# Due times in estimated nanoseconds, not in instruction numbers, for the order of the engines around TensorE

## Chip, core and metric

The kernel runs on one core of a Trainium2 chip. The metric is the device time of one execution in microseconds (us); lower is better. TensorE (PE in the profile; PEld is its weight load) has its instructions in the order of the program; VectorE is DVE, ScalarE is ACT, GpSimd is POOL, and SyncE (SP) issues all DMAs.

## What is computed

One step of a two-layer streaming encoder for 2048 new frames (the prompt) and 8 running streams of 16 frames. Layer A is a gated DeltaNet with 8 heads, layer B is RWKV-7 with 16 heads of 64. Both have a large input projection, a recurrence over time that is evaluated in blocks, and an output projection:

```python
h = rms_norm(x, norm_w[i])
# layer A
proj = h @ w_in                                   # 1024 -> 6160
qkv = silu(causal_conv(proj[..., :CONV_CH]))
o, s = gated_delta_rule(q, k, v, beta, g, s0)     # S_t = a_t S + k_t u_t^T
y = (rms_norm(o) * silu(z)) @ w_out               # 2048 -> 1024
# layer B
xs = h + (h_shifted - h) * mu                     # six mixes
r, k, v, z = xs[:4] @ w_in                        # 4 x (1024 -> 1024)
S = S * w_t + sa * b_t + v_t * k_t                # per head, per frame
y = ((group_norm(o) + bonus) * silu(z)) @ w_out
x = x + y
```

## The kernel before

**Tiling.** Tokens lie along the free dimension, channels along the 128 partitions. Layer A goes through five blocks of tokens (384 or 512 columns; the first holds the 8 running streams too), layer B through six (384 columns, the first 256). Each large product is made in 32-bit through splits: a weight pair `whl` and an activation pair hold a rounded part and the rest, and three matmuls replace one (L451 to L453 in layer A's input projection, L1059 to L1061 in layer B's, L168 to L170 in both output projections). ACT rounds (`L124` for weights, `L162` for activations), and DVE or POOL subtracts (`L125`, `L163`). A weight pair that is made once is stored to DRAM (`wd`, L128) and loaded from there for later blocks (`load_w`, L133); there are six slots for pairs of the input projections, two for those of the output projections.

**The order of TensorE** is written out by hand. Generators for the projection (the stream), the recurrences and the output projection are interleaved by `weave` and `rounds`, step by step: while TensorE goes through the projection of a later block, the small matmuls of the recurrences stand between. In layer B a step handles one pair of heads in 12 rounds: `b_prep`, `b_subst` (a 16x16 triangular inverse on DVE, 30 dependent operations at L842 and L844, then two hops through DRAM, `sc2b<-TB` and `cm<-sc2b`), `b_inverse` (POOL spreads the hopped blocks into `T`, L1265; matmuls at L1281 and on), `b_scan` (the recurrence: matmul L1390, DVE `XV` at L1392, matmul L1379 of the next chunk), `b_gate`, `b_out`. Layer A has the same parts (`T` at L655, first used at L705; the triangular merges down to L744). The transition, in which layer A's last heads run beside layer B's first projections, lies between.

**The order of the other engines** is left to a planner. `MANUAL` (L33) keeps TensorE in program order. For DVE, ACT, POOL and SP the planner runs through the program on a clock of its own, and each time an engine is free it takes, of the instructions that are ready then, the one with the lowest priority number; the lists that come out are then executed in order on the chip. The priority numbers come from `_due` (L1580). The program is built twice: the first time `note` (L1627) writes a log of all instructions, `_due` goes through the log from its end, and in the second build L1631 sets `tc.cur_priority` to each instruction's due.

In `_due`, a matmul that stands as number j in the log has due j. Any other instruction is due at the smallest of: its own number plus `SLACK` (300); the `need` of what it writes; the `free` of the buffers that it holds up (the due of the instruction that writes the next tile of the ring). Whoever feeds an instruction must be `LEAD` (6) numbers earlier, or `LEAD_DMA` (40) where the instruction is a DMA. So time is counted in instructions of all engines, whatever each takes.

Of the kernel before, what the change touches and what calls it, by code (L numbers as in the profile page):

```python
# [10 lines left out]
F32R = mybir.dt.float32r  # L11
AF = mybir.ActivationFunctionType
ALU = mybir.AluOpType
# [3 lines left out]
P = 128  # L17
# [13 lines left out]
WRAW, WHL = {"w": 3, "o": 2}, {"w": 6, "o": 2}  # L31
PSUM = {"mm": 2, "g": 3, "o": 1, "r": 2}
MANUAL = {mybir.EngineType.PE}  # L33
LEAD, LEAD_DMA, SLACK = 6, 40, 300
AHEAD, PACE, LAST_PACE, ROUNDS = 101, 17, 8, 12
EXPC = 0.5 * math.exp(-0.5)
B_BO, B_MK, B_MS, B_M16, B_B4, CB_W = 0, 128, 384, 448, 512, 516
# [1535 lines left out]
@with_exitstack  # L1573
def tile_hybrid_gdn_rwkv7_stream_step(ctx: ExitStack, tc: tile.TileContext, io: dict):
    k = _K(ctx, tc, io)
    k.setup()
    k.layers()


def _due(log):  # L1580


    ring, before, first = {}, {}, {}
    for j, (_, _, outs, _) in enumerate(log):
        for name, tag, bufs in outs:
            if tag is not None and name not in first:
                first[name] = j
                r = ring.setdefault(tag, [])
                r.append(name)
                if bufs and len(r) > bufs:  # L1590
                    before[name] = r[-1 - bufs]
    need, free, due = {}, {}, [0] * len(log)
    for j in range(len(log) - 1, -1, -1):
        engine, dma, outs, ins = log[j]
        wrote = [o[0] for o in outs]
        if engine == mybir.EngineType.PE:
            d = j
        else:
            d = min([j + SLACK] + [need[t] for t in wrote if t in need] + [free[t] for t in ins + wrote if t in free])
        due[j] = max(0, d + LEAD_DMA)  # L1600
        d -= LEAD_DMA if dma else LEAD
        for t in ins + [t for t in wrote if first.get(t) != j]:
            need[t] = min(need.get(t, d), d)
        for t in wrote:
            if first.get(t) == j and t in before:
                free[before[t]] = min(free.get(before[t], d), d)
    return due


def _build(arrays, due=None):  # L1610

    import concourse.bacc as _bacc

    nc = _bacc.Bacc("TRN2", target_bir_lowering=False, num_devices=1)
    io = {}
    for name, a in arrays.items():
        io[name] = nc.dram_tensor(f"in_{name}", a.shape, mybir.dt.from_np(a.dtype), kind="ExternalInput").ap()
    for name, shape in _OUTS.items():
        io[name] = nc.dram_tensor(f"out_{name}", shape, F32, kind="ExternalOutput").ap()
    log = []  # L1620

    def tiles(aps):
        ts = [getattr(getattr(a, "bass_ap", None), "tensor", None) for a in aps]
        return [(t.name, getattr(t, "tag", None), getattr(getattr(t, "tag_meta", None), "bufs", None)) for t in ts if t is not None]

    with tile.TileContext(nc) as tc:
        def note(inst, *_):  # L1627
            if due is None:
                log.append((inst.engine, "DMA" in type(inst).__name__, tiles(inst.outs), [t[0] for t in tiles(inst.ins)]))
            else:  # L1630
                tc.cur_priority = due[len(log)]  # L1631
                log.append(None)

        nc.push_inst_callback(note)
        tile_hybrid_gdn_rwkv7_stream_step(tc, io)
        nc.pop_inst_callback()
    return nc, log
# [31 lines left out]
```

## Time and profile before

| what | value |
|---|---|
| time, median of 3 runs | 4665.8 us (4654.6 to 4667.97) |
| the profiled execution, its own time | 4661.34 us |
| its span, first to last instruction | 4659.5 us |
| mean granted TensorE clock, share of full speed | 0.955 |
| PE busy | 4343.3 us, 93% |
| DVE busy | 3470.7 us, 74% |
| ACT busy | 2290.0 us, 49% |
| POOL busy | 1735.8 us, 37% |

A busy share is a mean over the whole span. TensorE's order is fixed, so its time is its matmuls, at the clock that is granted, and its waits.

### The profile page before, as it was taken

The numbers are of one execution on the slowest core, as the hardware profiler recorded it, in microseconds if no ns is written. First come the engines' busy times: TensorE is split into PE (matmuls) and PEld (weight loads), VectorE is DVE, ScalarE is ACT, GpSimd is POOL, SyncE is SP. The second block draws the span as 40 slices with busy tenths as digits, with TensorE's granted clock in tenths as the row PEclk, the third lists the DMA queues.
The fourth block names the chain that finished last, engine by engine and source line by source line (L and its number), as shares of the span: only waits on it lengthen the run. The fifth ranks groups of instructions, "written<-read, shape, count | busy, mean of one in ns | idle before, by whom it ended". The sixth has DMA issues, their size and how long they took to land. (4 is left out here: it accounts for less than half of the span.)

```text
span 4659.5 us, 104081 instructions
## 1 busy us (share of the span) xinstructions
PE 4343.3 (93%) x37093; PEld 3733.9 (80%) x37093; DVE 3470.7 (74%) x9203; ACT 2290.0 (49%) x6132; POOL 1735.8 (37%) x2507
## 2 busy tenths in 40 slices
PE   7999999999999999999987889999999999999996
PEld 6788788888888899999986767778787887887775
DVE  6778766686666766767678888877778778777784
ACT  5444544554434444444456655555545446445542
POOL 6555443332111211211103455444434434344441
PEclk8888999999999999999998989999999999999997
DMA  5555665555555666666655666766665665665442
GB/s 189 183 179 177 221 211 177 180 188 157 174 145 146 182 206 185 191 209 185 188 153 173 202 204 215 225 189 188 193 199 162 203 203 165 202 194 148 139 131 70
DMA packets 765670, 842.18 MB, mean 181 GB/s; under 512 B 263480, under 2 KB 497360, under 8 KB 765152
## 3 DMA queue, kind: packets, MB, share of 16 engines
q1 hardware_dynamic: 765152, 835.53, 59.5%
q8 instruction: 294, 4.82, 0.4%
q14 instruction: 224, 1.84, 0.1%
HBM read 632.73 MB, written 202.53 MB: 179 GB/s over the span
## 5 line engine op out<-in xcount | busy, mean ns | idle before, releaser
L451 PE MATMUL ps<-hh,whl 128*128 128x384 f32 (+1 forms) x1960 | 804.7, 411 | 12.4 <-ACT hh L162 10.3
L452 PE MATMUL ps<-hl,whl 128*128 128x384 f32 (+1 forms) x1960 | 718.2, 366 | 2.5 <-DVE hl L163 2.0
L453 PE MATMUL ps<-hh,whl 128*128 128x384 f32 (+1 forms) x1960 | 717.3, 366 | 2.7 <-POOL whl L125 2.7
L1059 PE MATMUL ps<-xh,whl 128*128 128x384 f32 (+1 forms) x1632 | 608.4, 373 | 32.8 <-ACT xh L162 19.0
L1060 PE MATMUL ps<-xl,whl 128*128 128x384 f32 (+1 forms) x1632 | 561.1, 344 | 21.3 <-POOL xl L163 12.4
L1061 PE MATMUL ps<-xh,whl 128*128 128x384 f32 (+1 forms) x1632 | 559.3, 343 | 9.9 <-DVE whl L125 9.6
L125 POOL TENSOR_TENSOR whl<-wraw,whl 128x256 fp32r<-128x256 f32 x454 | 365.9, 811 | 414.4 <-ACT whl L124 389.8
L571 DVE SCALAR_TENSOR_TENSOR cv<-pre,cw,cv 128x512 f32<-128x512 f32 (+3 forms) x576 | 375.3, 659 | 124.8 <-ACT cv L569 117.8
L124 ACT CAST whl<-wraw 128x256 fp32r<-128x256 f32 x726 | 287.8, 402 | 313.2 <-PE ps L453 94.4
L451 PEld LDWEIGHTS ps<-hh,whl 128*128 128x128 f32 x1960 | 377.4, 193 | 69.3 <-issue 18.5
L168 PE MATMUL ps<-oh,whl 128*128 128x384 f32 (+2 forms) x1024 | 392.1, 383 | 27.7 <-DMA whl<-wd 14.9
L453 PEld LDWEIGHTS ps<-hh,whl 128*128 128x128 f32 x1960 | 376.5, 192 | 39.6 <-POOL whl L125 4.2
L452 PEld LDWEIGHTS ps<-hl,whl 128*128 128x128 f32 x1960 | 378.2, 193 | 35.4 <-DVE hl L163 5.8
L1059 PEld LDWEIGHTS ps<-xh,whl 128*128 128x128 f32 x1632 | 322.1, 197 | 76.4 <-ACT xh L162 25.3
L169 PE MATMUL ps<-ol,whl 128*128 128x384 f32 (+2 forms) x1024 | 368.5, 360 | 6.9 <-DVE ol L163 6.7
L170 PE MATMUL ps<-oh,whl 128*128 128x384 f32 (+2 forms) x1024 | 365.3, 357 | 0.7 <-POOL whl L125 0.7
L842 DVE TENSOR_TENSOR sbt<-B,TB 48x15 f32<-48x15 f32 (+14 forms) x1320 | 346.5, 262 | 23.6 <-DMA B<-scr 2.8
L844 DVE TENSOR_TENSOR TB<-TB,sbt 48x15 f32<-48x15 f32 (+14 forms) x1320 | 347.6, 263 | 19.6
L1060 PEld LDWEIGHTS ps<-xl,whl 128*128 128x128 f32 x1632 | 325.1, 199 | 33.1 <-POOL xl L163 16.8
L1061 PEld LDWEIGHTS ps<-xh,whl 128*128 128x128 f32 x1632 | 323.6, 198 | 18.4 <-DVE whl L125 17.8
L820 DVE TENSOR_TENSOR x<-x,ps 128x384 f32<-128x384 f32 (+1 forms) x320 | 191.3, 598 | 91.1 <-PE ps L170 90.7
L168 PEld LDWEIGHTS ps<-oh,whl 128*128 128x128 f32 x1024 | 198.7, 194 | 66.6 <-ACT oh L162 9.6
(349 smaller groups left out, 10268.4 us busy)
## 6 DMA issues: line engine op xcount, KB each, us to landing
whl<-wd SPq DMA_DIRECT2D x1582, 256.0 KB
wd<-whl SPq DMA_DIRECT2D x428, 256.0 KB
wraw<-in_w_a SPq DMA_DIRECT2D x288, 128.0 KB
wraw<-in_w_b SPq DMA_DIRECT2D x256, 128.0 KB
kvd<-kvo SPq DMA_DIRECT2D x160, 192.0 KB
xn<-x1d SPq DMA_DIRECT2D x80, 192.0 KB
wraw<-in_w_ao SPq DMA_DIRECT2D x96, 128.0 KB
xn<-in_x SPq DMA_DIRECT2D x32, 256.0 KB
```

The source lines that it names most:

```text
L125: (self.nc.gpsimd if tag == "o" else self.weng).tensor_tensor(w[:, 1], raw, w[:, 0].bitcast(F32), op=SUB)
L168: self.nc.tensor.matmul(out, lhsT=wh, rhs=hh, start=first and i == 0, stop=False)
L169: self.nc.tensor.matmul(out, lhsT=wh, rhs=hl, start=False, stop=False)
L170: self.nc.tensor.matmul(out, lhsT=wl, rhs=hh, start=False, stop=i == n - 1)
L451: nc.tensor.matmul(p, lhsT=wh[:, k % 2], rhs=hh, start=k == 0, stop=False)
L452: nc.tensor.matmul(p, lhsT=wh[:, k % 2], rhs=hl, start=False, stop=False)
L453: nc.tensor.matmul(p, lhsT=wl[:, k % 2], rhs=hh, start=False, stop=k == KT - 1)
L571: nc.vector.scalar_tensor_tensor(o, f(j), self.cw[:, ct, j:j + 1], o, op0=MUL, op1=ADD)
L844: nc.vector.tensor_tensor(T[:, j + 1:16, 0:j + 1], T[:, j + 1:16, 0:j + 1], o, op=SUB)
L1059: nc.tensor.matmul(o, lhsT=wh[:, i], rhs=xh, start=k == 0, stop=False)
L1060: nc.tensor.matmul(o, lhsT=wh[:, i], rhs=xl, start=False, stop=False)
L1061: nc.tensor.matmul(o, lhsT=wl[:, i], rhs=xh, start=False, stop=k == KT - 1)
```

## The change

`LEAD_DMA` goes. Each log entry now carries an estimated duration in nanoseconds (`_cost`): for DVE, ACT and POOL a constant and a rate per element of a partition, with 1200 more for a power; for a DMA 4000 and 0.04 per element; for a matmul 0.46 per column in the split products, else by its size. The matmuls' estimated durations added up give a clock (`at`); a matmul's due is its place on that clock. Any other instruction's due is the smallest of its place plus 40,000 ns, the needs and the frees, less its own duration, so it is a latest start. What feeds a matmul must be 1000 ns ahead of it; what feeds another instruction must be done at that one's latest start. Where dues below zero were cut off at zero, all dues are now shifted so that the smallest is zero. Nothing else differs: the same instructions, tiles, buffers and TensorE order.

```diff
-LEAD, LEAD_DMA, SLACK = 6, 40, 300
+LEAD, SLACK = 1000, 40000
+DMA_COST, POW_COST = (4000, 0.04), 1200
+COST = {mybir.EngineType.DVE: (280, 0.95), mybir.EngineType.Activation: (250, 1.0), mybir.EngineType.Pool: (300, 2.2)}
...
+def _cost(inst):
+
+    outs, ins = [[tuple(p.shape) for p in (getattr(a, "bass_ap", None) for a in aps) if p is not None] for aps in (inst.outs, inst.ins)]
+    if "DMA" in type(inst).__name__:
+        return DMA_COST[0] + DMA_COST[1] * max([math.prod(s) for s in outs + ins] + [0])
+    n = max([math.prod(s[1:]) for s in outs + ins] + [1])
+    if inst.engine != mybir.EngineType.PE:
+        a, b = COST.get(inst.engine, (100, 0))
+        return a + b * n + (POW_COST if getattr(inst, "op", None) == ALU.pow else 0)
+    k, m = ins[1][0], math.prod(ins[1][1:])
+    n = math.prod(ins[0][1:])
+    if ins[0] and inst.ins[0].bass_ap.dtype == F32R:
+        return 0.46 * n
+    return max(30 + 1.5 * n * k * m / (P * P), 200 if k * m == P * P else 0)
...
+    at, now = [], 0.0
+    for engine, cost, _, _ in log:
+        at.append(now)
+        now += cost if engine == mybir.EngineType.PE else 0
...
-        engine, dma, outs, ins = log[j]
+        engine, cost, outs, ins = log[j]
...
         if engine == mybir.EngineType.PE:
-            d = j
+            d = at[j]
         else:
-            d = min([j + SLACK] + [need[t] for t in wrote if t in need] + [free[t] for t in ins + wrote if t in free])
-        due[j] = max(0, d + LEAD_DMA)
-        d -= LEAD_DMA if dma else LEAD
+            d = min([at[j] + SLACK] + [need[t] for t in wrote if t in need] + [free[t] for t in ins + wrote if t in free]) - cost
+        due[j] = d
+        if engine == mybir.EngineType.PE:
+            d -= LEAD
...
-    return due
+    low = min(due)
+    return [int(d - low) for d in due]
...
-                log.append((inst.engine, "DMA" in type(inst).__name__, tiles(inst.outs), [t[0] for t in tiles(inst.ins)]))
+                log.append((inst.engine, _cost(inst), tiles(inst.outs), [t[0] for t in tiles(inst.ins)]))
```

## Rows read from the trace of the kernel before

**Rows 1.** The page's head: span, and busy time of each engine.

```profile
span 4659.5 us, 104081 instructions
...
PE 4343.3 (93%) x37093; PEld 3733.9 (80%) x37093; DVE 3470.7 (74%) x9203; ACT 2290.0 (49%) x6132; POOL 1735.8 (37%) x2507
```

**Rows 2.** Busy time and granted clock in five stretches of the span.

```profile
core 0: us, PE busy (x) PEld busy (x) DVE busy (x) ACT busy (x) POOL busy (x), PEclk, DMA share, GB/s
0.00:500.00 500.00, 448.12 (x2470) 388.12 (x2471) 379.46 (x982) 239.59 (x654) 289.60 (x488) 0.89 0.58 185
500.00:2330.00 1830.00, 1798.15 (x11049) 1572.61 (x11048) 1267.99 (x3238) 815.54 (x2047) 456.96 (x741) 1.00 0.61 183
2330.00:2800.00 470.00, 396.81 (x3168) 335.46 (x3166) 380.31 (x1168) 285.93 (x824) 178.32 (x285) 0.90 0.59 183
2800.00:4543.00 1743.00, 1620.81 (x19433) 1373.56 (x19433) 1384.85 (x3663) 914.26 (x2496) 789.32 (x965) 0.95 0.63 184
4543.00:4660.00 117.00, 79.43 (x986) 64.14 (x982) 58.09 (x157) 34.69 (x112) 21.62 (x28) 0.78 0.24 70
```

**Rows 3.** Waits of PE: whom for, us in total, times, longest.

```profile
PE ps L1379 <- DVE XV L1392: 43.7, 38, 2.6
PE ps L744 <- DVE T L739: 22.3, 18, 1.4
...
PE ps L1281 <- POOL T L1265: 17.5, 5, 7.3
...
PE ps L1060 <- POOL xl L163: 12.4, 12, 4.1
...
PE ps L705 <- POOL T L655: 7.9, 2, 6.5
...
PE ps L106 <- POOL OC L1473: 5.2, 1, 5.2
PE ps L1185 <- POOL ch L1158: 4.2, 2, 3.6
```

**Rows 4.** Timeline of one wait in layer B, in order of start.

```profile
4276.05 3.48 POOL L1178 TENSOR_TENSOR BK<-ch,ch 64x384 f32<-64x384 f32 x3
...
4278.58 1.24 DVE L1099 TENSOR_TENSOR w<-w2r,w 64x256 fp32r<-64x256 f32 x1
...
4279.85 0.60 DVE L1392 SCALAR_TENSOR_TENSOR XV<-ps,wc,Sw 64x64 f32<-64x64 f32 x2
...
4280.18 0.59 PE L1379 MATMUL ps<-XV,GM 128*64 128x64 f32 x3 [2.27 <-DVE XV L1392]
```

**Rows 5.** Busy times and granted clock just after that wait.

```profile
4281.80:4288.60 6.80, 6.80 (x70) 5.22 (x68) 4.55 (x19) 1.47 (x5) 0.83 (x1) 0.50 0.23 62
```

**Rows 6.** The chain of waits in layer B: start, us, what.

```profile
3588.38 0.17 PE ps L1059
...
3588.90 1.54 PE ps L1281 x48
```

**Rows 7.** Instruction groups by shape: busy us, mean ns, idle before.

```profile
L842 DVE TENSOR_TENSOR sbt<-B,TB 48x15 f32<-48x15 f32 x80 | 23.5, 294 | 2.4 <-DMA B<-scrb 1.3
...
L1392 DVE SCALAR_TENSOR_TENSOR XV<-ps,wc,Sw 64x64 f32<-64x64 f32 x416 | 116.6, 280 | 82.2 <-PE ps L1390 70.8 <-PE ps L1395 3.3
...
L1265 POOL TENSOR_TENSOR T<-cm,cb 128x384 f32<-128x384 f32 x80 | 67.8, 855 | 125.3 <-DMA cm<-sc2b 76.8 <-PE ps L1345 35.8 <-DVE GM L1213 4.1
```

**Rows 8.** DMAs on the chain of waits in layer B: start, us from issue to landing.

```profile
3441.53 4.54 DMA whl<-wd
...
3622.53 3.60 DMA cm<-sc2b
...
4323.90 4.13 DMA sc2b<-TB
```

**Rows 9.** Waits of SP's DMA queue, the longest in total.

```profile
SPq L133 <- PE ps L453: 528.6, 453, 3.2
```

**Rows 10.** One DVE line: duration ns min/median/max, first and last start.

```profile
L1099 DVE TENSOR_TENSOR w<-w2r,w x48: 421/976/1416, 2491.2 to 4463.3; 64x256 fp32r<-64x256 f32 x48
```

## Prediction

> **What bounds the kernel now.** I read the page's head first. TensorE is busy for 4343.3 of 4659.5 us and DVE, the next, for 3470.7 [rows 1]. So no other engine sets the time by its sum; the time is TensorE's fixed list, plus its waits of 4659.5 - 4343.3 = 316 us, plus what a lowered clock costs. The table by stretches says where these lie [rows 2]. Span less PE busy gives 52 us of idle time up to 500 us (layer A's first block), 32 in the long rest of layer A, 73 in the transition, 122 in layer B, 38 at the end. Its PEclk column, one minus it times the length, gives 55, 0, 47, 87 and 26 us of clock lost, 215 in all. Layer A after 500 us is therefore full: 1798 of 1830 us at full clock. All that another order can gain lies in the other four stretches.
>
> The two losses go together. Before the matmul at 4280.18 us TensorE waited 2.27 us [rows 4], and in the stretch from 4281.8 to 4288.6 us, in which it was busy throughout, the granted clock was 0.50 of full speed, 1.2 GHz in place of 2.4 [rows 5]. Over the span 215 us of clock go with 316 us of waits, so I count 0.68 us of clock for each us of wait that is saved or added, which is an estimate from these two sums.
>
> Then whom TensorE waits for [rows 3]. The costliest single wait is on `XV` (43.7 us in 38 times), the step of layer B's recurrence. POOL is waited for in five rows: `T` 17.5 and 7.9, `xl` 12.4, `OC` 5.2, `ch` 4.2, 47.2 us together, which is much for an engine that is busy 37% of the span [rows 1]. An engine that is free so often and is yet waited for has done its work in the wrong order, or got its input late. The wait on L739 (22.3 us in 18 times, never over 1.4) is of another kind: a matmul, a copy and the next matmul, with too little between; an order can't shorten that.
>
> **The change part by part.** It adds and removes no instruction, so busy sums stay, and TensorE's list stays. What moves is the order on DVE, ACT, POOL and SP, and only where the planner has more than one instruction ready.
>
> *The unit.* Without DMAs there are 26,557 instructions in layer B's 1743 us, 15.2 per us, and 17,075 in the 1830 us of full layer A, 9.3 per us [rows 2]. The old lead of 6 numbers is thus 0.39 us in layer B and 0.64 us in layer A on average, and it stretches and shrinks: split matmuls start each 0.17 us, so 6 of them take 1.0 us, while 48 small matmuls take 1.54 us, so 6 of those take 0.19 us [rows 6]. Behind such a burst the old rule gives nearly no lead, and layer B's recurrence and inverse are made of bursts.
>
> *DVE and ACT.* The new price of `XV` is 280 + 0.95 x 64 = 341 ns (it took 280), that of a 48x15 step of the inverse 294 ns (it took 294) [rows 7]. With the 1000 ns before the matmul, `XV` must start 1.34 us ahead of its matmul where it was due 0.39 us ahead. But in the wait that I looked at, DVE ran `w` (1.24 us) for a matmul of the next step when `XV` became ready [rows 4]; no due helps if `XV` was not ready when `w` was picked. Bounds: nothing, and half of the 43.7 us. I take a quarter, 10.9 us, since most of its waits are a single operation long (43.7 / 38 = 1.15 us).
>
> *POOL.* 384 elements now cost 300 + 2.2 x 384 = 1145 ns (`T` took 855 [rows 7]) against 0.39 us: here the old price was furthest off, two to three times too low. Work that feeds TensorE through POOL gets its place earlier by about 0.75 us for each POOL step. Bounds: nothing, and all of the 47.2 us. Some of it is a late DMA before the POOL operation, since `T` sat idle 76.8 us for `cm` [rows 7]. I take half, 23.6 us.
>
> *SP and the hops.* A hop of `cm` is priced at 4000 + 0.04 x 12,288 = 4.5 us (it took 3.60), the one of `sc2b` at 5.0 (4.13), a load of a weight pair at 4000 + 0.04 x 65,536 = 6.6 us (4.54) [rows 8]; each was 40 numbers, 2.6 us in layer B. The chain of `subst` (30 steps, a copy, two hops, `T`) was due to start some 272 numbers, 18 us, ahead of its matmul; now it is 9.7 + 0.5 + 9.5 + 1.1 + 1.0 = 22 us. That helps the waits on `T` and stands in the POOL term. Against it, a load is now ordered by its latest start, 7.6 us before its matmul, and a `cm` hop 6.6 us before that of `T`; before, the hop was 6 numbers (0.4 us) ahead of the load. Loads overtake hops. SP stands at L133 1.17 us at a time until TensorE frees a slot (528.6 / 453 [rows 9]), and all that is behind it stands too. Bounds: nothing, and two such waits (`sc2b`, `cm`) in each of layer B's 48 pairs of heads, 2 x 1.17 x 48 = 112 us. I take nothing, because the waits of `T` on TensorE's side are 5 in number [rows 3] and the hops start 4 us earlier; the upper end is a rival below.
>
> *At no cost.* The shift to a smallest due of zero changes no order but at the start, where 52 us of idle time are all there is. The slack goes from 300 numbers, 25 us at 54,935 instructions in 4659.5 us [rows 1], to 40 us: it postpones stores that nobody needs, and a store that holds a buffer is still bound by its `free`. If that cover went, it would show as SP's waits.
>
> *The sum.* 10.9 + 23.6 = 34.5 us of waits, with clock 34.5 x 1.68 = 58 us: 4661.3 - 58 = 4603 us on the profiled run's clock. That run lies 4.5 us under the median of the runs, so I say 4605 us, 1.3% faster.
>
> **A rule against it.** DVE's `w` has two inputs in SBUF, and one shape took 421, 976 and 1416 ns (least, median, most) [rows 10]; in the wait above it took 1.24 us beside a POOL operation that ran from 4276.05 to 4279.53 [rows 4]. The Trainium skill (SBUF — State Buffer, Who interferes with whom) says that a DVE instruction with two SBUF inputs contends with a GpSimd instruction that reads SBUF, and that the second one is blocked for the whole instruction. By that rule no fixed price per element fits DVE; the trace agrees, as the price for 256 elements is 523 ns. What it would make of the time is the third rival.
>
> **The rivals.**
> 1. *Nothing to pick.* With one instruction ready at a time the due doesn't matter; the wait at 4280 is of that kind, and DVE's 74% leave room. Against it: POOL's 47 us. The order still shifts a little and the time ends within 14 us of before: 4666.
> 2. *Loads ahead of hops.* A third of the 112 us reaches TensorE, since `T` is now the longest chain into it: 37 x 1.68 = 63 us, 4661 + 63 = 4724, and with the 4.5 us 4728, slower. It decides from 34.5 us on, where it eats the gains. For it: 76.8 us that POOL already sits for `cm`; against it: only 17.5 of them get to TensorE.
> 3. *DVE prices too low where POOL runs.* POOL's work moves earlier, into stretches where DVE is due; operations take 1.24 us that are priced 0.52, and `XV` stands behind them. If its waits double (43.7 us) and POOL's half is gained, 20.1 us are added, x 1.68 = 34: 4700, slower. It decides from 23.6 us of added DVE waits on.
>
> **How the numbers follow.** My forecast has 0.50, its own range 4545 (all of POOL's waits and half of `XV`'s: 69 x 1.68 = 116 us) to 4651. Rival 1 has 0.21, rival 2 0.17, rival 3 0.12. A measurement of this kernel can't tell less than about 0.3%, 14 us, from no change. Faster by more than that has 0.51 (a little of rival 1's edge), within it 0.20, slower 0.29. The range for 8 in 10 is 4530 to 4725: a little under the forecast's best case, up to most of rival 2.
>
> **What would show it.** Right: POOL's five rows of waits fall from 47 to about 24 us, `XV` to some 33, PE idle to about 280 us, mean clock above 0.955 with the gain in the transition and layer B, and the stretch from 500 to 2330 us of the same length within 10 us. Wrong: `T` <- `cm` waits rise on POOL and on TensorE (rival 2); mean durations of DVE's two-input operations rise with waits on `XV` (rival 3); the same rows with the same counts (rival 1). Wrong altogether if the long layer A stretch opens up, where TensorE waits little now and so has 32 us to win and much to lose.

## The result, and the profile after

The changed kernel took 4682.4 us (median of 6 runs, 4675.2 to 4690.7), the kernel before beside it 4662.5 us (6 runs, 4648.4 to 4668.0). The ratio is 1.0051, with a 95% interval of 1.0032 to 1.0071: half a per cent slower, where 1.3% faster was predicted. Run once more beside other kernels (e8) it gave 1.0050 (1.0033 to 1.0066). The profiled execution took 4690.7 us.

The head of its page, to set beside [rows 1]:

```profile
span 4688.9 us, 104185 instructions
...
PE 4335.9 (92%) x37093; PEld 3739.2 (80%) x37093; DVE 3481.4 (74%) x9203; ACT 2290.3 (49%) x6132; POOL 1719.0 (37%) x2507
```

The list of work is the same. Span less PE busy was 316 us and is now 353. Two of the five stretches of [rows 2]:

```profile
core 0: us, PE busy (x) PEld busy (x) DVE busy (x) ACT busy (x) POOL busy (x), PEclk, DMA share, GB/s
...
500.00:2330.00 1830.00, 1811.08 (x11073) 1583.57 (x11072) 1258.78 (x3241) 812.81 (x2047) 448.49 (x740) 0.99 0.61 183
2330.00:2800.00 470.00, 372.86 (x3044) 322.85 (x3042) 367.97 (x1119) 274.60 (x795) 160.39 (x266) 0.88 0.57 178
...
```

In the transition PE is busy for 24 us less than before in the same 470 us and gets through 3044 matmul records where it got through 3168. The waits of PE over the whole span, whose names answer to those of [rows 3] (every line number is two higher):

```profile
PE ps L1381 <- DVE XV L1394: 47.5, 44, 2.6
PE ps L1283 <- POOL T L1267: 31.3, 7, 7.8
PE ps L1436 <- DVE VS L1407: 18.5, 10, 2.8
PE ps L1062 <- POOL xl L165: 16.4, 9, 4.2
PE ps L889 <- DVE TB L846: 15.9, 5, 4.1
...
PE ps L1187 <- POOL ch L1160: 14.2, 4, 6.5
PE ps L170 <- ACT oh L164: 12.6, 11, 1.4
PE ps L746 <- DVE T L741: 11.0, 17, 4.1
PE ps L707 <- POOL T L657: 10.7, 2, 9.6
...
PE ps L1061 <- ACT xh L164: 6.8, 6, 2.2
```

and before, the rows that [rows 3] leaves out:

```profile
PE ps L1059 <- ACT xh L162: 19.0, 16, 2.4
...
PE ps L1061 <- DVE whl L125: 9.6, 20, 1.2
...
PE ps L1434 <- DVE VS L1405: 7.8, 4, 2.5
...
PE ps L887 <- DVE TB L844: 3.6, 1, 3.6
...
PE ps L168 <- ACT oh L162: 3.5, 6, 1.2
```

Four rows on POOL rose (`T` 17.5 to 31.3 and 7.9 to 10.7, `xl` 12.4 to 16.4, `ch` 4.2 to 14.2), and `XV` rose by 3.8. Three rows on other engines rose by as much together: `TB` by 12.3, `VS` by 10.7, `oh` by 9.1. Of the rows above 9 us three fell to less than half: `xh` (19.0 to 6.8) and `whl` (9.6 to 0.2), the inputs and the weights of layer B's projection, and the one on L741, of which the prediction said that no order could shorten it. In a second execution of the changed kernel (e8) each of the rows shown lies within 3 us of these.

TensorE's list of work being the same, the two traces can be laid on each other: for each matmul, when it started less when the same matmul started before. The growth of that difference in seven stages (bounds in time of the kernel before), for all kernels of this study, from one profiled execution each:

```
us won (-) or lost (+)  6-683 683-2327 2327-2453 2453-2683 2683-2963 2963-3547 3547-4651
changed kernel          +10.5    -17.4      -1.9     +31.3      +0.4     -10.3     +16.5
the same, again (e8)     -2.9    -17.5      +2.1     +28.1      -1.7      -9.5     +12.3
e1 ring out              +6.7    -18.0      +3.9     +10.4     +10.0      -7.2     +12.6
e2 before, long lead     -2.9     +5.4      +4.6     +20.6      -2.8      -3.6      +4.7
e3 load 10 us           +10.3    -15.2      +1.2     +26.1      +1.7     -10.0     +15.9
e4 equal prices          -1.7     -6.4      +2.0      +9.1     +10.1     -12.8     +10.3
e5 loads early          +10.3    -16.9      +1.8     +21.1     +20.7      -8.8     +13.1
e6 casts early           +9.1    -15.5      +2.8     +21.7      -1.2      -9.4     +15.9
e7 two orders            +7.1    -15.0      +3.4      +1.7      +7.4     -10.1     +10.0
e9 late reductions       +4.0    -16.4      -0.6      -0.1      -0.7      -2.4      +6.8
e10 prices on numbers    +6.2    -18.3      +3.7      +7.5      -5.0     -15.6      -4.0
e11 window               -4.2    -16.6      -0.3      +1.9      -3.0      -9.7      +5.0
e12 measured axis, out   -0.1    -17.6      -0.6      +3.3      -0.1     -10.1     +22.3
e13 measured axis        -8.3    -13.6      +1.1     +11.8      -2.5      -8.5     +11.7
```

The two rows of the same kernel show how far one execution can be read: 1 to 4 us in most stages, 13 in the first. Three more runs test this: behind 2453 us, e9 and e11 have the order of before on every engine, and so has e2 from 3547 us on. What their rows show there, -9.7 to +6.8 us, isn't order. All three show a loss in the last stage (+4.7 to +6.8), so the profiled execution of before was itself some 5 us short there. The profiled executions of e4, e8 and e13 were the shortest of their 12, that of e5 the longest of 6, so the sum of a row isn't the ratio. The stages before 683 and after 2963 say little alone. Two stages are clear: **the steady part of layer A wins 17 us, and 2453 to 2683 us, layer B's first chunks, loses 28 to 31.**

**The gain.** DVE's timeline around the copies of one step of the inverse, before (start, duration, line, operation):

```profile
1646.15 0.54 DVE L621 TENSOR_REDUCE sm<-QT 128x3 f32<-128x384 f32 x1
1646.73 0.25 DVE L738 TENSOR_SCALAR T<-ps 32x96 f32<-32x96 f32 x1
1647.01 0.27 DVE L622 TENSOR_SCALAR sm<-sm 128x3 f32<-128x3 f32 x1
1647.31 0.25 DVE L739 TENSOR_SCALAR T<-ps 32x96 f32<-32x96 f32 x1
...
1648.16 0.26 DVE L739 TENSOR_SCALAR T<-ps 32x96 f32<-32x96 f32 x1
```

and after:

```profile
1650.72 0.25 DVE L740 TENSOR_SCALAR T<-ps 32x96 f32<-32x96 f32 x1
1650.98 0.24 DVE L741 TENSOR_SCALAR T<-ps 32x96 f32<-32x96 f32 x1
1651.24 0.26 DVE L740 TENSOR_SCALAR T<-ps 32x96 f32<-32x96 f32 x1
1651.52 0.26 DVE L741 TENSOR_SCALAR T<-ps 32x96 f32<-32x96 f32 x1
...
1652.93 0.55 DVE L623 TENSOR_REDUCE sm<-QT 128x3 f32<-128x384 f32 x1
```

Four copies that TensorE waits for had the small operations of another chain laid between them, from 1646.73 to 1648.42; now they run through in 1.06 us.

**The loss.** PE's waits in 2453 to 2640 us after:

```profile
PE ps L1187 <- POOL ch L1160: 12.8, 2, 6.5
PE ps L1122 <- DVE w L1101: 8.2, 1, 8.2
PE ps L1283 <- POOL T L1267: 7.8, 1, 7.8
PE ps L1061 <- ACT xh L164: 6.8, 6, 2.2
```

Before, the wait on `w` was there too (8.7), `T` had 4.9 and `ch` nothing. One of the two waits on `ch` on ACT's timeline after, up to the operation that POOL's `ch` needs:

```profile
2521.38 0.39 ACT L126 CAST whl<-wraw 128x256 fp32r<-128x256 f32 x1
2521.67 0.69 ACT L1010 ACTIVATE xt<-H,mu 128x128 f32<-128x128 f32 x2
2522.27 0.40 ACT L126 CAST whl<-wraw 128x256 fp32r<-128x256 f32 x1
2522.56 0.41 ACT L164 CAST xh<-xt 128x256 fp32r<-128x256 f32 x1
2522.87 0.51 ACT L1153 ACTIVATE ch<-K,prm 128x256 f32<-128x256 f32 x1
```

The same `ch<-K` ran at 2514.07 before. What stands ahead of it now are casts of weights and of the inputs of coming matmuls. TensorE isn't ready for many of these weights: ACT's waits in 2440 to 2650 us after begin with

```profile
ACT whl L126 <- PE ps L1063: 26.7, 25, 4.5
ACT whl L126 <- DMA wraw<-in_w_b: 20.4, 20, 3.2
```

where ACT's casts before waited 1.7 us for TensorE, and for their loads

```profile
ACT whl L124 <- DMA wraw<-in_w_b: 33.6, 35, 2.0
```

A cast that waits for TensorE has its data and wants a buffer that TensorE still reads: it came too early, and ACT stood with all that was behind it.

**A first theory.** `_due` passes a due time back through a ring of buffers as well (`free`). A raw weight load is now priced at 4000 + 0.04 x 32,768 = 5.3 us, its cast and subtraction at half a us each: 6.3 us for one trip round three buffers. TensorE uses three pairs there in some 2 us of the planner's axis, so each trip puts loads and casts 4 us further ahead of need. Worked out with the kernel's own planner, the due of a cast lies 56 us (median), at most 112, ahead of its place in layer B's first block, and was behind it before. The rival theories: other prices put layer B's chains late, or the early loads themselves stand in SP's queue (the prediction's second rival).

### The profile page after: what moved, and what is told of

It is laid out like the page before. It is cut to its first block, busy times and chain, and to the rows that moved or that the text cites. A ratio compares the mean times of both kernels' runs of the same rounds, so it can differ in the third digit from the quotient of the medians.

```text
span 4688.9 us, 104185 instructions
## 1 busy us (share of the span) xinstructions
PE 4335.9 (92%) x37093; PEld 3739.2 (80%) x37093; DVE 3481.4 (74%) x9203; ACT 2290.3 (49%) x6132; POOL 1719.0 (37%) x2507
## 5 line engine op out<-in xcount | busy, mean ns | idle before, releaser
L1062 PE MATMUL ps<-xl,whl 128*128 128x384 f32 (+1 forms) x1632 | 558.0, 342 | 23.0 <-POOL xl L165 16.4
L844 DVE TENSOR_TENSOR sbt<-B,TB 48x15 f32<-48x15 f32 (+14 forms) x1320 | 356.6, 270 | 37.2 <-DMA B<-scr 12.4
L846 DVE TENSOR_TENSOR TB<-TB,sbt 48x15 f32<-48x15 f32 (+14 forms) x1320 | 346.8, 263 | 22.3
L1062 PEld LDWEIGHTS ps<-xl,whl 128*128 128x128 f32 x1632 | 323.4, 198 | 31.0 <-POOL xl L165 19.2
```

The costliest lines, as they stand in the source:

```text
L844: nc.vector.tensor_tensor(o, B[:, j + 1:16, j:j + 1].to_broadcast([rows, m, j + 1]), T[:, j:j + 1, 0:j + 1].to_broadcast([rows, m, j + 1]) ...
L846: nc.vector.tensor_tensor(T[:, j + 1:16, 0:j + 1], T[:, j + 1:16, 0:j + 1], o, op=SUB)
L1062: nc.tensor.matmul(o, lhsT=wh[:, i], rhs=xl, start=False, stop=False)
```

## The experiments

**e1, the raw ring out of the dues.** In `_due`, behind the ring's bookkeeping:

```diff
-                if bufs and len(r) > bufs:
+                if bufs and len(r) > bufs and not tag.startswith(("wraw", "oraw")):
```

> The changed kernel, but the ring of raw weight buffers (3 of them, 2 for the output weights) passes no due time back from one weight pair to the pair three before it. Theory (the chain of dues through that ring): with the change a weight load is priced at 5.3 us, so each trip round the three buffers pushes the dues of loads and casts 6.3 us further ahead where TensorE uses three pairs in some 2 us; the due of a cast lay 56 us (median) and up to 112 us ahead of its place in layer B's first block, 41 and 91 us in the kernel's first stretch. Without it these leads are -4 us. The 31 us that the change lost between 2453 and 2635 us come back (25 to 31), the 17 us won in the steady part of layer A stay: 4645 to 4660 us, ratio to before 0.995 to 0.999; the waits of ACT's casts on TensorE's accumulators of L1063 (26.7 us in 2440 to 2650) fall under 10. Rival (other prices, of the chains from LoRA to the first hop, put these chains late): the loss stays, 4676 to 4688 us.

Ratio 1.0027 (1.0013 to 1.0041). The loss of 2453 to 2683 falls from 28 to 31 us to 10.4, but 10.0 more are lost up to 2963. ACT's casts still wait for TensorE:

```profile
ACT whl L126 <- PE ps L1063: 12.0, 9, 5.4
```

By the ratio about half of the loss comes back. The ring is a cause, and not the whole one: the theory's numbers are missed. The 4679.6 us lie among the rival's, but the kernel before took 4669.8 us beside it; on the 4662.5 us of the first result the ratio gives 4675, just under them.

**e2, the ring's lead alone, in the kernel before.**

```diff
-        d -= LEAD_DMA if dma else LEAD
+        d -= (90 if wrote[0].startswith("wraw") else LEAD_DMA) if dma else LEAD
```

> The kernel before, with its instruction numbers, but a load into a raw weight buffer leads its cast by 90 numbers, not by 40: three pairs then take 102 numbers round the ring, and the due of a cast in layer B's first block lies 409 numbers (median), at most 1126, ahead of its place, about the 56 and 112 us of the changed kernel at some 10 numbers to a microsecond; it was 96 behind. Theory of the ring: this alone makes the transition slower as the change did, by 20 to 35 us between 2453 and 2635, so 4680 to 4700 us in all, without the 17 us won in layer A. Rival (other prices): within 6 us of before.

4690.3 us, ratio 1.0055 (1.0033 to 1.0076), 20.6 us lost in the stage. One trip round the three buffers is 102 numbers there, where it was 52. ACT's wait on a buffer is back as well, with nothing else changed:

```profile
ACT whl L124 <- PE ps L1061: 23.2, 17, 6.6
```

A raw load whose lead is too long round its ring is enough by itself to make layer B's start slow.

**e3, a dearer load.** Raw loads at 10,000 ns.

> The changed kernel with a raw weight load priced at 10 us in place of 5.3: a trip round the three buffers then pushes 11 us, and the dues of casts lie 287 us (median), up to 420 us ahead in layer B's first block, and 100 to 520 us ahead for the reloads before it. Theory of the ring: the casts win over everything for longer, the transition loses more than with 5.3 us: 4690 to 4730 us. If the loss was already whole at 56 us ahead (a cast that is ahead by more than what waits beside it can't be put further ahead), 4680 to 4690. Rival (other prices): 4682 within 6 us.

4692.6 us, ratio 1.0059 (1.0038 to 1.0079), 26.1 us lost in the stage: not to be told from the changed kernel. By the ring's theory the loss is then whole at 56 us of lead; by the rival the price does nothing. This run tells for neither.

**e4, the new axis with equal prices.** e1 with these lines changed:

```diff
-        return DMA_COST[0] + DMA_COST[1] * max([math.prod(s) for s in outs + ins] + [0])
+        return 3840
...
-        return a + b * n + (POW_COST if getattr(inst, "op", None) == ALU.pow else 0)
+        return 576
...
-LEAD, SLACK = 1000, 40000
+LEAD, SLACK = 576, 40000
```

> The changed kernel with its axis of TensorE time, but with the old prices turned into time: 576 ns for every operation of another engine, 3840 ns for a transfer, 576 ns after a matmul, whatever the shape (6, 40 and 6 numbers of 96 ns), and the ring of raw weight buffers kept out as in the first experiment. Theory A (the 17 us of the steady part of layer A come from prices by engine and shape, which put the four copies of 128x512 ahead of the small reductions): that gain goes, and the kernel is within 6 us of before, 4657 to 4669 us. Theory B (they come from the axis in time): the gain stays, within 6 us of the first experiment.

Ratio 1.0041 (1.0027 to 1.0055). The gain of layer A falls from 17 to 6.4 us, which is theory A; but the kernel isn't at the time of before, since 19.2 us are lost between 2453 and 2963. With the raw ring out and the prices equal, what is left of the change there is the axis, and the slack of 40 us.

**e5 and e6, early loads or early casts alone.** Both sets of dues are worked out, the ring in and out; e5 takes the first for SP and the second for the other engines, e6 the reverse:

```diff
+    ring, free = _dues(log), _dues(log, ("wraw", "oraw"))
+    due = [r if l[0] == mybir.EngineType.SP else f for l, r, f in zip(log, ring, free)]
```

> The changed kernel with the dues of its transfers (SP) as they are, those into raw weight buffers some 55 to 111 us ahead in layer B's first block, but every operation of ACT, DVE and POOL with the dues of the kernel without the raw ring's chain: the loads are early, the casts aren't. Theory C (the casts, put ahead of the chains on ACT and DVE, are what TensorE waits for): as the first experiment, 12 us lost between 2453 and 2635, ratio to before 1.001 to 1.004. Theory D (the loads, put ahead of the hops and reloads on SP's queue, the second rival of the prediction): as the changed kernel, 25 to 31 us lost there, ratio 1.004 to 1.007.

> The reverse: transfers with the dues of the kernel without the raw ring's chain (loads -2 us ahead), operations of ACT, DVE and POOL with the dues of the changed kernel (casts 56 us ahead, up to 112). Theory C (the casts): 25 to 31 us lost between 2453 and 2635, ratio to before 1.004 to 1.007. Theory D (the loads): 12 us lost there, ratio 1.001 to 1.004. If both are needed (a cast can't run before its load), this one and the one with early loads both lose 12.

Ratios 1.0063 (1.0042 to 1.0084) and 1.0041 (1.0024 to 1.0058); 21.1 and 21.7 us lost in the stage, and with early loads another 20.7 behind it. None of the three cases foreseen: either alone costs most of it there. Two of PE's waits in 2440 to 2660 us with early loads:

```profile
PE ps L1283 <- POOL T L1267: 14.6, 2, 7.9
...
PE ps L1063 <- DVE whl L127: 9.7, 13, 1.9
```

the longest with early casts:

```profile
PE ps L1283 <- POOL T L1267: 11.6, 1, 11.6
```

and the same two before:

```profile
PE ps L1061 <- DVE whl L125: 8.0, 14, 1.2
...
PE ps L1281 <- POOL T L1265: 4.9, 2, 4.4
```

So the weights come hardly later than before; what comes later in both kernels is `T`, whose tables come over two hops on SP's queue. POOL's waits for these hops in the same window are 0.3 us before and 14.2 with early loads, but also 15.3 with early casts,

```profile
POOL TB L838 <- DMA sc2b<-TB: 8.8, 2, 5.1
POOL T L1267 <- DMA cm<-sc2b: 6.5, 2, 5.0
```

18.5 in the changed kernel and 12.5 with the ring out (e1). Late hops are there, as the prediction's second rival has it, but with and without early loads: that the loads make them late isn't shown. What is shown is that the dues of SP alone, e5 against e1, add 21 us between 2453 and 2963 in these two executions.

**e7, two orders in one kernel.** The changed kernel's dues (ring out) up to number 20,000, the old rule's behind it, read off on one axis:

```diff
+HYBRID = 20000
...
+    old = [at[max(0, min(d, len(at) - 1))] for d in old]
+    due = [n if j < HYBRID else o for j, (n, o) in enumerate(zip(new, old))]
```

> Two orders in one kernel: the first 20000 of 48538 instructions of the program (layer A up to its last blocks) take the dues of the changed kernel without the raw ring's chain, the others those of the kernel before (6, 40 and 300 numbers), read off at the same axis of TensorE time. If the gain of the steady part of layer A and the loss behind it are separate, the 17 us are won and nothing is given back: 4645 to 4655 us where before has 4662 to 4670, ratio 0.996 to 0.998. If a shorter layer A is lost again in the transition (something other than TensorE sets it, as the transfers or DVE), 0.999 to 1.001.

Ratio 0.9992 (0.9978 to 1.0007): no difference, which is the second of the two cases foreseen. The stage behaves (1.7 us lost), layer A's gain is there (15.0), but 7.1 us are lost ahead of it and 7.4 behind, as far as one execution tells. On this axis old dues that fall between two matmuls are equal, and the lists of DVE, ACT, POOL and SP differ from those of before there, so this run can't say that a shorter layer A is lost again; e11 is the cleaner test.

**e8**, the changed kernel once more, is the second row of the table.

> The changed kernel once more, beside the others on one chip: ratio to before 1.003 to 1.007; 25 to 31 us lost between 2453 and 2635, 14 to 18 us won between 683 and 2327.

**e9, five operations moved.** The kernel before, with a later due for five operations of each head and chunk group:

```diff
+    late = set()
+    for j, (engine, _, outs, ins) in enumerate(log):
+        if engine == mybir.EngineType.DVE and ins and outs[0][0].startswith("sm_") and ins[0].startswith("QT_"):
+            late.update(range(j - 1, j + 4))
...
-        due[j] = max(0, d + LEAD_DMA)
+        due[j] = max(0, d + LEAD_DMA) + (70 if j in late else 0)
```

> The kernel before, with one thing moved: for each head and chunk group of layer A the five operations of L620 to L624 (the product with the identity, the reduction and the three small ones behind it) get a due time 70 numbers later, so that they stand behind the four copies of L738 and L739 as in the changed kernel (before, their dues are 15609 to 15633 in a case where those of the copies are 15655 to 15678). Theory (this one exchange is the gain of the steady part of layer A): 12 to 18 us won between 683 and 2327, and since nothing else moves, 4646 to 4656 us where before has 4662, ratio 0.996 to 0.998. If the gain comes from other moves as well, 3 to 10 us there, ratio 0.998 to 1.000.

4647.8 us, ratio 0.9979 (0.9964 to 0.9994), 16.4 us won in layer A; in the stages behind, which have the order of before, the row stays within the spread. PE's wait on the copies in 683 to 2330 us is in this kernel

```profile
PE ps L744 <- DVE T L739: 5.5, 16, 0.9
```

against

```profile
PE ps L744 <- DVE T L739: 19.7, 16, 1.4
```

before, 5.4 us in 15 times in the changed kernel and 16.7 in 15 with equal prices (e4). That one exchange is layer A's gain, and it comes from the prices.

**e10, the prices by shape on instruction numbers.** No axis in time and no latest starts; transfers 40 numbers, a matmul 6, slack 300, as before:

```diff
-            d = at[j]
+            d = j
...
-            d = min([at[j] + SLACK] + [need[t] for t in wrote if t in need] + [free[t] for t in ins + wrote if t in free]) - cost
+            d = min([j + 300] + [need[t] for t in wrote if t in need] + [free[t] for t in ins + wrote if t in free])
         due[j] = d
...
+        d -= 6 if engine == mybir.EngineType.PE else 40 if engine == mybir.EngineType.SP else cost / 96
```

> The other half of the change alone: dues counted in instruction numbers as before, 40 numbers for a transfer, 6 after a matmul, slack 300, but every operation of DVE, ACT and POOL priced by engine and shape (the changed kernel's nanoseconds over 96 ns a number). Three pairs round the raw ring then take 50 numbers as before, so no lead piles up. Theory: the gain of layer A comes from these prices (12 to 18 us between 683 and 2327), the loss of 2453 to 2683 from the ring and from the axis in time, so it is under 6 us here: ratio 0.996 to 0.999. Rival (prices by shape also put the chains of layer B late): 10 us or more lost between 2453 and 2683, ratio 0.999 to 1.003.

4643.7 us, ratio 0.9966 (0.9950 to 0.9982): faster than before. 18.3 us won in layer A, 7.5 lost in 2453 to 2683 (a little over the 6 foreseen, under the rival's 10) and 5.0 of these won back by 2963. The longest waits of PE in this kernel:

```profile
PE ps L1381 <- DVE XV L1394: 42.1, 38, 2.7
PE ps L1283 <- POOL T L1267: 24.8, 9, 7.4
```

`XV` waits as in [rows 3] and `T` 7.3 us more: right prices shorten neither.

**e11, the window.** As e7, but the new dues hold from number 5800 to 20,000 alone (some 620 to 2190 us), and every instruction of another engine moves the axis on by 0.01 ns, so that no two old dues are equal.

> As the kernel with two orders, but the changed kernel's dues (without the raw ring's chain) hold from number 5800 to 20000 alone, some 620 to 2190 us, behind the first chunks of layer A where that kernel still lost 7 us, and the order of all the rest is exactly that of before. 12 to 16 us won and kept: ratio 0.9965 to 0.998. If the clock or another stage takes it back, 0.998 to 1.000.

4633.9 us against 4653.8, ratio 0.9945 (0.9926 to 0.9963): the best of the study. Its windows:

```profile
500.00:2330.00 1830.00, 1804.60 (x11147) 1580.41 (x11146) 1268.33 (x3272) 818.59 (x2067) 453.85 (x744) 1.00 0.62 184
2330.00:2800.00 470.00, 403.65 (x3299) 340.58 (x3299) 389.34 (x1196) 288.86 (x836) 185.81 (x294) 0.91 0.60 187
```

11147 matmul records in the steady stretch where there were 11049 [rows 2], at the same clock, and the transition isn't held up. Its 16.6 us of layer A are 0.36%, and the ratio is some 9 us better than that. The granted clock goes with the surplus: a median of 0.9585 over the six runs of e11, of 0.956 over the 21 of before and 0.9555 over the 12 of e9. Among those 21 runs of one kernel, 0.001 of clock goes with some 2.7 us, so 0.0025 would be some 7 us, an estimate. Whether this order earns the clock or six runs had it by chance, no run shows.

**e12 and e13, an axis that was measured.** What e1 and e4 still lose in 2453 to 2963 led to a second theory. The new axis counts TensorE's estimated durations and nothing else:

```
from the trace before     numbers   time that passed   PE busy   axis of the changed kernel
480 to 2360 us              17011            1880 us   1838 us                      1827 us
2440 to 2720 us              3293             280 us    237 us                       176 us
3000 to 4520 us             18199            1520 us   1421 us                      1158 us
```

In the second stretch 280 us are 176 on the axis. Of the 104 us that it lacks there, 43 are TensorE's idle time and 61 are matmuls that took longer than their price, in part at a lowered clock:

```profile
2440.00:2720.00 280.00, 237.08 (x2012) 198.11 (x2011) 234.94 (x738) 171.15 (x501) 121.14 (x209) 0.90 0.61 192
```

In layer B it is 99 and 263. So the axis is short less by the waits that it leaves out than by prices of matmuls that are too low. A chain priced at 10 us is put 10 us of axis ahead of its matmul, which is 16 us of real time in the transition, and the longer a chain or the more trips round a ring, the further too early it stands. In e12 and e13 the axis is a table of the times at which the kernel before reached each number; in e12 the raw ring is out.

```diff
-    for engine, cost, _, _ in log:
-        at.append(now)
-        now += cost if engine == mybir.EngineType.PE else 0
+    for (a, s), (b, e) in zip(AXIS, AXIS[1:]):
+        at += [1000 * (s + (e - s) * (j - a) / (b - a)) for j in range(a, b)]
```

> The kernel of the first experiment (prices by shape, raw ring kept out), but its axis isn't the sum of TensorE's estimated durations (176 us of axis for the 280 us that run from 2440 to 2720, 1827 for the 1880 us of the steady part of layer A): it is the time at which the kernel before reached each number, a table of 116 points 40 us apart from its trace. Theory (that axis runs short where TensorE doesn't set the pace, so that the leads of the long chains in layer B's first chunks reach too far ahead): the 20 us that the first experiment still lost between 2453 and 2963 fall under 8, the gain of layer A stays: ratio 0.994 to 0.998. Rival (the axis isn't it): 1.001 to 1.004.

> The changed kernel with that measured axis and nothing else: the raw ring is back in, at 5.3 us a load. On this axis three pairs have more time, and the lead of a cast in layer B's first block is -4 us (median), 13 at most, in place of 56 and 112; in the stretch just before it is still 34, 66 at most (148 and 184). Theory (ring and axis are one fault: an axis that is short of time, against which the ring's trips pile up): the loss of 2453 to 2683 falls from 28 to 31 us to 5 to 12, ratio 0.995 to 0.999. Rival (the ring's price costs as before wherever it leads at all): 20 us or more lost there, ratio 1.002 to 1.005.

e12: ratio 0.9998 (0.9983 to 1.0014), against 1.0027 for e1. Of the 20.4 us that e1 loses between 2453 and 2963, 3.2 are left, as the theory has it. (The table of e12 has a point every 40 us and between them advances evenly with instruction numbers. So it brings back real time from stage to stage and the even steps of the numbers inside them; no run tells these two apart.) The ratio misses its range, since 22.3 us are lost in the last stage. e13: ratio 1.0021 (1.0006 to 1.0035) against 1.0050 for the changed kernel; the stage loses 11.8 us in place of 28 to 31, within the theory's range, and ACT's casts wait

```profile
ACT whl L126 <- PE ps L1063: 11.9, 11, 4.4
```

in place of 26.7. Its ratio too is above what was expected; the profiled execution (4652.7 us) was the shortest of its 12 (median 4670.2), so its row in the table flatters it.

## Why the prediction was wrong

The ratios put together: prices by shape alone 0.9966; the rest of the change with them, the raw ring out, 1.0027; the ring in, 1.0050. So 0.3% was won by the prices, 0.6% lost with the axis in time (and the latest starts, leads, slack and prices of transfers that come with it), 0.2% lost with the ring. On the measured axis the ring costs the same 0.2% (0.9998 to 1.0021), and the rest 0.3% less; where the other 0.3% goes isn't shown. Each of these differences is good to about 0.2%, so the ring's is only just clear, though it was found twice.

- **The unit** is the step that failed. The prediction took time for the better unit, because a number "stretches and shrinks". It didn't ask what the new unit was time of. The axis is the sum of TensorE's estimates: it runs at 0.97 of real time in layer A and at 0.63 in the transition, 1.5 times apart. The numbers count every engine's instructions: 9.0 per us in layer A and 11.8 in the transition, 1.3 times apart, so from stage to stage they were the truer clock. (The prediction's 15.2 and 9.3 per us were counted from trace records, 37,093 for the 26,571 matmuls of the planner's list; that list has 48,538 entries, 10.4 per us of the run.) e4, with equal prices and the ring out, loses 19.2 us between 2453 and 2963 with this axis; e12 against e1 shows that another axis takes 17 of e1's 20 us away.
- **SP and the hops**, and what came "at no cost": `free` is named once, for stores. A load's price was weighed against a hop's and never followed round its own ring of three buffers, where it counts again on every trip. e2 shows that this alone can cost 20 us; in the stage the changed kernel loses 18 to 21 us more than e1 without the ring, and e13 loses 8.5 more than e12.
- **The wait on L739**, "an order can't shorten that": it fell from 19.7 to 5.4 us in the steady part of layer A, and e9 shows that the exchange behind it is the gain there. The mean wait of a single operation's length was read as a bare dependency; DVE's timeline would have shown another head's reductions between the copies. The sign named for it, the long layer A stretch of the same length within 10 us, came out wrong to the good side, by 17.
- **The sum**: POOL's five rows were to fall by 23.6 us and rose by 30.6, from 47.2 to 77.8 (31.3 + 16.4 + 14.2 + 10.7 + 5.2); `XV` was to fall by 10.9 and rose by 3.8. Where the prices act alone (e10) `XV` stays within 1.6 us and POOL's five rows are 47.5 us (24.8 + 12.1 + 5.2 + 4.1 + 1.3): `xl` and `ch` fall by 11.2, the two `T` rise by 11.5. So both terms were nothing on balance. (The sum itself, 4603 + 4.5, is 4607.5 and not 4605, which changes nothing.)
- **0.68 us of clock for each us of wait** held for the clock and not for the time. PE's idle time rose by 37 us, and the mean granted clock went from 0.955 to 0.950, which by the prediction's own count (one minus the clock, times the span) is 25 us more, 0.68 for each us of wait. But the span rose by 29 us and not by 62, since the busy time fell by 7: clock that is lost by this count needn't be time.
- **The rivals.** "Nothing to pick" is refuted by both clear stages. "Loads ahead of hops" is half borne out: early loads cost some 20 us (41.8 in e5 between 2453 and 2963, 20.4 in e1), and its sign came true, `T` waiting longer for `cm` on POOL (77.1 to 83.4 us) and TensorE for `T`. But the hops are late without early loads as well (e6), and its place, two waits in every pair of heads, didn't come. "DVE prices too low where POOL runs" is refuted: DVE's busy time moved by 11 us in 3471, `w` got faster, not slower (below), and `XV` waits as before. The time lies in the range of 4530 to 4725 us only because the rivals stretched it upward.

**Open:** with dues in time every kernel loses 10 to 22 us behind 3547 us; with the order of before there the rows show +5 to +7, so some 4 to 16 of it is the order, and e10 gains by some 10. The measured axis doesn't cure it, so the axis being short isn't the cause. No run splits it further. Open too is why e11 ran at a higher clock, and why either half of the early work (e5, e6) costs nearly the whole.

## What to carry to other kernels

A planner that counts back from one engine's work needs an axis that advances as time does; the sum of that engine's estimated work ran at 0.63 of it in one stage here, through prices that were too low and waits that it left out. Lay the plan's axis beside the trace in each stage first. Then follow every new price round each ring of buffers: if a trip costs more than the consumer takes for that many buffers, the lead grows with every trip until early work blocks the engines. And a wait on a short operation is only a bare dependency if the producer's timeline shows nothing of another chain between its input and it.

## What was not expected of the hardware

The same DVE instruction, `w`, has the same shape and place in both kernels, but [rows 10] had a median of 976 ns and after it is

```profile
L1101 DVE TENSOR_TENSOR w<-w2r,w x48: 422/424/1278, 2491.0 to 4481.9; 64x256 fp32r<-64x256 f32 x48
```

Sorted by whether a POOL instruction ran beside it for over 0.1 us: before, 33 of the 48 did and took 1141 ns in the median, the other 15 took 422; after, 25 with 955 and 23 with 423. The median of all 48 halved as 8 fewer ran beside POOL, which none of the planner's prices knows of. The Trainium skill (SBUF — State Buffer, Who interferes with whom) has it that a DVE instruction with two SBUF inputs contends with a GpSimd instruction that reads SBUF. The two medians agree with that; what it says of the reason, no run here shows.
